# State products four in a row, a contiguous tap table stored from ScalarE's queue, and whole 128x128 turns of the state-space layer's input

## The chip, the cores and the metric

The kernel runs on one core of one Trainium2 chip. The metric is the device time of one execution in microseconds. The engines are named as in the profile: PE is TensorE's matmuls and PEld its weight loads, DVE is VectorE, ACT is ScalarE, POOL is GpSimd, and SP is SyncE, which only issues DMAs here. A name with a q (ACTq, SPq) is the engine's queue of waits and DMA issues.

## What is computed

The program is a two-layer sequence model on 1024 tokens of 1024 features, in float32: an RWKV-7 layer, an MLP, a diagonal state-space layer (S5) with GELU and a gated linear unit, and an MLP, with a LayerNorm behind each. The change is in the S5 layer, which has 64 groups of 16 features, each with a complex diagonal state of 64:

```python
bu_re = einsum('tbgc,gpc->tbgp', u_c, bbar_re)      # input products
bu_im = einsum('tbgc,gpc->tbgp', u_c, bbar_im)
# s_t = abar * s_(t-1) + bu_t, complex, one abar for each group and state
y = einsum('tbgp,gcp->tbgc', s_re, cr_w) - einsum('tbgp,gcp->tbgc', s_im, ci_w)
y = gelu(y + x * d_skip)
z = y @ w_glu
out = z[..., :d] * sigmoid(z[..., d:])
```

## The kernel before

**Layout and order.** Features lie on the 128 partitions, in 8 tiles; the tokens are halved, and `hA` and `hB` are the 8 tiles of 512 tokens of either half. All large products (the MLPs, the projections, the gate) go through `dense`: each float32 weight tile comes by DMA (`wraw`), ScalarE casts it to a high part (`whi`, L148), VectorE subtracts the rest (`wlo`, L149), and TensorE does three products per block (L188). The text calls this dense work. A list scheduler orders each engine's instructions by rank (`tc.cur_priority`): the S5 layer's steps have ranks from 99000 to 99500, the MLPs 200000. So while S5 of one half waits for something, dense work of the MLP of the other half goes first in TensorE's row. PSUM tiles come from four pools: `pd` (3 buffers, dense work), `pl` (1), `pa` (2) and `pc` (2).

**S5 in blocks of 8 tokens.** The recurrence is unrolled over blocks of 8 tokens, so that a half has 64 blocks (`NSC`) and a group's 16 features by 8 tokens fill 128 rows. `s5_tables` works out three tables for each of the 8 feature tiles, once, and stores them in DRAM: `tB` (input of a block to the state at its end), `tC` (state at a block's start to the block's outputs) and `tT`, the taps (inputs of a block to outputs of the same block). The taps of a tile are worked out in `pk`, copied by ScalarE into `kpad` behind zeros (L1155), and stored by SP with one overlapping read for each parity (L1159); a group's parity (`par`) is whether it is even or odd.

`s5(H, h)` then runs for each half in three stages.

- Input stage, by pairs of feature tiles (`f2` of 4): the tile's tokens are turned, 64 blocks at a time, by `turn` (L154 is a product by the identity, L156 a transpose), copied to `u1`, turned back by groups (L1195) to `ug`, multiplied by `tB` (L1206) and copied into the states `hb`.
- Scan: `advance` on VectorE and GpSimd, over `hb`.
- Output stage, by the same pairs: for each parity, the taps (L1250) and the state products (L1255) add into one PSUM tile `py`; ScalarE copies it to `y1` (L1257); TensorE turns it to features by tokens (`pyt`, L1263); VectorE adds the skip term (L1265) into `yg`, which has one buffer; ScalarE does GELU (L1267), and SP stores it to DRAM, where `glu` reads it.

A transpose writes a product's operand times the identity. In names such as `py<-tcm,hb 64*64 64x128`, `tcm` is the operand that moves through the array and `hb` the one loaded as weights, 64 rows by 64 columns; a product's column half follows from the output's partitions.

## Time and profile before

| | us |
|---|---|
| median of 3 runs | 2743.06 (2741.53 to 2747.41) |
| the profiled execution | 2746.6 |
| its span in the trace | 2744.8 |
| S5 tables | about 1070 to 1275 |
| first half: input stage, scan, output stage | about 1325 to 1410, 1410 to 1484, 1484 to 1540 |
| second half: input stage, scan, output stage | about 1858 to 1935, 1935 to 2010, 2010 to 2069 |

The span is that of the profiled execution from its first to its last instruction. The stages' ends are read from the timeline, where the first half's work begins and ends; dense work runs in all of them.

### The profile page before, as it was taken

The numbers are of one execution on the slowest core, as the hardware profiler recorded it, in microseconds if no ns is written. First come the engines' busy times: TensorE is split into PE (matmuls) and PEld (weight loads), VectorE is DVE, ScalarE is ACT, GpSimd is POOL, SyncE is SP. The second block draws the span as 40 slices with busy tenths as digits, with TensorE's granted clock in tenths as the row PEclk, the third lists the DMA queues.
The fourth block names the chain that finished last, engine by engine and source line by source line (L and its number), as shares of the span: only waits on it lengthen the run. The fifth ranks groups of instructions, "written<-read, shape, count | busy, mean of one in ns | idle before, by whom it ended". The sixth has DMA issues, their size and how long they took to land.

```text
span 2744.8 us, 43807 instructions
## 1 busy us (share of the span) xinstructions
PE 2598.4 (95%) x16582; PEld 2089.9 (76%) x16582; DVE 1813.3 (66%) x3191; ACT 1154.8 (42%) x2038; POOL 630.6 (23%) x515
## 2 busy tenths in 40 slices
PE   7999979989899999989999999999999999999997
PEld 5778757678677777767876788778778887788886
DVE  7477677577786867997567553674855546755556
ACT  7455574544543333353532332434223324433334
POOL 3121542432442122342122000120220101210101
PEclk9989979999899999999999999999999999999998
DMA  4765455564223334545333533233343322333333
GB/s 146 235 214 175 151 164 156 178 203 142 81 86 88 93 92 148 141 129 163 100 112 127 174 95 100 81 96 112 103 164 110 96 96 81 119 96 96 96 96 100
DMA packets 215058, 345.90 MB, mean 126 GB/s; under 512 B 21184, under 2 KB 75584, under 8 KB 214848
## 3 DMA queue, kind: packets, MB, share of 16 engines
q1 hardware_dynamic: 214848, 343.10, 40.5%
q8 instruction: 131, 2.15, 0.3%
q14 instruction: 79, 0.65, 0.1%
HBM read 279.06 MB, written 63.96 MB: 125 GB/s over the span
## 4 chain that ended last, share of the span: by engine, by line
PE 44%; DVE 4%; issue 3%; DMA 1%; POOL 1%; ACT 1%; ACTq 0%; SPq 0%; DVEq 0%; POOLq 0%
PE d L188 39%; PE py L1250 1%; PE py L1255 1%; DVE wlo L149 1%; DMA wraw<-in_mw_dram 1%; PE pu L154 1%; PE pbu L1206 1%; POOL rl L975 1%; DVE hA L991 0%; DMA s_y<-yg 0%; DVE t L1218 0%; DVE hB L991 0%; ACT whi L148 0%; DVE sq L876 0%; PE pu L1195 0%
## 5 line engine op out<-in xcount | busy, mean ns | idle before, releaser
L148 ACT CAST whi<-wraw 128x512 fp32r<-128x512 f32 x668 | 413.5, 620 | 929.1 <-PE d L188 623.2
L149 DVE TENSOR_TENSOR wlo<-wraw,whi 128x512 fp32r<-128x512 f32 x668 | 500.6, 750 | 426.8 <-ACT whi L148 404.3
L188 PE MATMUL d<-qbuf,whi 128*128 128x512 f32 (+1 forms) x2112 | 657.0, 394 | 23.8 <-DVE hA L991 12.8
L188 PEld LDWEIGHTS d<-qbuf,whi 128*128 128x128 f32 x2112 | 391.8, 191 | 120.0 <-DVE hA L991 17.8
L188 PE MATMUL d<-qbuf,wlo 128*128 128x512 f32 (+1 forms) x1056 | 411.9, 392 | 10.7 <-DVE wlo L149 10.4
L975 POOL TENSOR_TENSOR rl<-rl 128x512 f32<-128x512 f32 x128 | 157.2, 1228 | 1094.5 <-ACT rl L974 1094.5
L188 PE MATMUL d<-oAh,whi 128*128 128x512 f32 (+1 forms) x960 | 390.9, 411 | 15.5 <-ACT ev L418 6.3
L188 PE MATMUL d<-oAl,whi 128*128 128x512 f32 (+1 forms) x960 | 387.5, 405 | 3.0 <-DVE oAl L149 2.8
L188 PE MATMUL d<-oAh,wlo 128*128 128x512 f32 (+1 forms) x960 | 386.5, 405 | 2.4 <-DVE wlo L149 2.3
L188 PE MATMUL d<-oBh,whi 128*128 128x512 f32 x704 | 279.2, 397 | 0.0
L188 PE MATMUL d<-oBh,wlo 128*128 128x512 f32 x704 | 278.7, 396 | 0.2 <-DVE wlo L149 0.2
L188 PE MATMUL d<-oBl,whi 128*128 128x512 f32 x704 | 277.1, 394 | 0.0
L188 PEld LDWEIGHTS d<-qbuf,wlo 128*128 128x128 f32 x1056 | 201.7, 191 | 56.5 <-DVE wlo L149 14.5
L188 PEld LDWEIGHTS d<-oAh,whi 128*128 128x128 f32 (+1 forms) x960 | 185.9, 194 | 62.2 <-ACT ev L418 8.4
L188 PEld LDWEIGHTS d<-oAh,wlo 128*128 128x128 f32 (+1 forms) x960 | 185.8, 194 | 44.4 <-DVE wlo L149 3.2
L188 PEld LDWEIGHTS d<-oAl,whi 128*128 128x128 f32 (+1 forms) x960 | 185.6, 194 | 43.1 <-DVE oAl L149 5.2
L991 DVE TENSOR_TENSOR hB<-hB,d 128x512 f32<-128x512 f32 (+1 forms) x256 | 165.0, 650 | 71.2 <-PE d L188 68.0
L991 DVE TENSOR_TENSOR hA<-hA,d 128x512 f32<-128x512 f32 x240 | 162.1, 682 | 64.4 <-PE d L188 62.1
L188 PEld LDWEIGHTS d<-oBh,wlo 128*128 128x128 f32 x704 | 132.9, 189 | 32.4 <-issue 2.0
L188 PEld LDWEIGHTS d<-oBl,whi 128*128 128x128 f32 x704 | 133.1, 189 | 29.9 <-issue 0.7
L188 PEld LDWEIGHTS d<-oBh,whi 128*128 128x128 f32 x704 | 133.1, 189 | 29.0 <-issue 1.2
L149 DVE TENSOR_TENSOR qbuf<-rl,qbuf 128x512 fp32r<-128x512 f32 x128 | 95.0, 742 | 73.5 <-ACT qbuf L148 73.5
(374 smaller groups left out, 3804.8 us busy)
## 6 DMA issues: line engine op xcount, KB each, us to landing
wraw<-in_mw_dram SPq DMA_DIRECT2D x520, 256.0 KB, 2.7
wraw<-in_glu_dram SPq DMA_DIRECT2D x64, 256.0 KB, 2.7
low<-wlo SPq DMA_DIRECT2D x52, 256.0 KB, 2.6
wlo<-low SPq DMA_DIRECT2D x52, 256.0 KB, 3.6
wraw<-in_wk_dram SPq DMA_DIRECT2D x32, 256.0 KB, 3.5
wraw<-in_wr_dram SPq DMA_DIRECT2D x32, 256.0 KB, 3.9
wraw<-in_wv_dram SPq DMA_DIRECT2D x32, 256.0 KB, 4.3
yl<-s_y SPq DMA_DIRECT2D x32, 256.0 KB, 3.1
```

What stands on the lines that cost most here:

```text
L148: S.copy(hi, src)
L149: (e or V).tensor_sub(lo, src, hi.bitcast(F32))
L154: PE.matmul(out, x, idt, start=True, stop=True)
L188: bulk.append((PE.matmul(p, w, x, **kw).ins, x.shape[-1]))
L975: G.tensor_mul(r, r, r)
L991: V.tensor_add(z, z, p)
L1206: PE.matmul(p[qs, g2, ri], tb[:, g2, ri, qs], u[:, 2 * g2 + par], start=True, stop=True)
L1250: PE.matmul(p[64 * j : 64 * j + 64, g2], ug[f][:, 2 * g2 + par], tv[:, par, g2], start=g2 == 0, stop=False, skip_group_check=True)
L1255: PE.matmul(p[64 * j : 64 * j + 64, g2], hb[qs, 4 * f + g2, ri, 0:NSC], tcm[qs, g2, ri], start=False, stop=ri == 1, skip_group_check=True)
```

## The change

It has four parts.

1. Input stage. Each tile of the pair is turned by four transposes of 128x128, with every fourth token in one (L1200 of the changed kernel); the way back is by products with a selection matrix `sel` of 128 x 2 x 64 that picks the even or the odd rows (L1207), 16 for each tile.
2. Tap table. `tT` has another layout, in which the 128 columns of a tap's moving operand lie one behind the other; before, they lay 4 elements apart. There are two `kpad` tiles, for four feature tiles each; the stores go out in two groups of 16, after the fourth and the eighth tile, and ScalarE's queue issues them (L1170) instead of SP's.
3. Output stage. Both parities have a PSUM tile at once, one from `pc` and one from `pa`. The taps of both come first (L1264). The state products (L1272) go by both parities and both tiles of the pair in turn, four on the four 64x64 quadrants of the array; `inorder` fixes this order.
4. `pyt` is taken from `pl` (1 buffer) instead of `pa` (2).

```diff
@@ -31,6 +31,7 @@
 LNG = (1, 3, 5)
 LNT = (2, 5)
 TB = 2
+TBF = 4
 LN8R = 400000
 MIXR = 100
 W0B = 5
@@ -126,6 +127,8 @@
     cmask = kp.tile([128, 8, L], F32, name="cmask")
     V.memset(cmask, 1.0)
     V.memset(cmask[:, :, 0:1], 0.0)
+    sel = cp.tile([128, 2, 64], F32, name="sel")
+    V.tensor_copy(sel, ident.rearrange("p (n e) -> p e n", e=2))
     mhalf = cp.tile([128, 64], F32, name="mhalf")
     V.memset(mhalf, -0.5)
 
@@ -180,6 +183,12 @@
                     SP.dma_start(low[key, k0], lo.bitcast(F32).rearrange("p k n -> p (k n)"))
             out += [(hi[:, k], lo[:, k]) for k in range(step)]
         return out
+
+    def inorder(prods):
+
+        for x, y in zip(prods, prods[1:]):
+            tc.add_manual_dep(y.ins, x.ins.name, mybir.DependencyInfo(
+                mybir.DependencyClass.NoSync, mybir.DependencyReason.DATA), reason="order")
 
     bulk, hops = [], []
     ST = getattr(nc, STE)
@@ -1019,7 +1028,7 @@
 
     SL = 8
     NSC = HT // SL
-    tT = dr.tile([KT, 128, 2, 512], F32, name="tT")
+    tT = dr.tile([128, 2, KT, 4, 128], F32, name="tT")
     tB = dr.tile([KT, 128, 4, 2, 128], F32, name="tB")
     tC = dr.tile([KT, 128, 4, 2, 128], F32, name="tC")
 
@@ -1102,10 +1111,12 @@
         V.tensor_sub(ci, ci, tq)
         V.tensor_mul(ci, ci, den)
 
-        kpad = pp.tile([128, 16, 16, 4], F32, name="kpad")
-        G.memset(kpad, 0.0)
+        kpads = [pp.tile([128, TBF, 4, 16, 16], F32, name=f"kpad{j}") for j in range(KT // TBF)]
+        for kpad in kpads:
+            G.memset(kpad[:, :, :, 0:8], 0.0)
         for f in range(KT):
             gs = slice(4 * f, 4 * f + 4)
+            kpad = kpads[f // TBF]
             bc = pp.tile([128, 2, 2, 4, 16], F32, tag="bc", name="bc", bufs=1)
             SP.dma_start(bc, A["s5bc"][f])
             bb = pp.tile([128, 2, 4, 16], F32, tag="bb", name="bb", bufs=1)
@@ -1152,11 +1163,13 @@
                                   ca[ps_, g2, ri, 0:8].rearrange("p t c -> p (t c)"), start=ri == 0, stop=ri == 1)
             for par in range(2):
                 ps_ = slice(64 * par, 64 * par + 16)
-                S.copy(kpad[ps_, 8:].rearrange("p t c g -> p g (t c)"), p[ps_])
-            tv = tT[f].rearrange("(s c) two n -> two c s n", c=16)
-            for par in range(2):
-                src = kpad[64 * par : 64 * par + 16, 1:9].rearrange("p t c g -> p (t c g)")
-                SP.dma_start(tv[par], bass.AP(src.tensor, src.offset, [src.ap[0], (64, SL), src.ap[1]]))
+                S.copy(kpad[ps_, f % TBF, :, 8:].rearrange("p g t c -> p g (t c)"), p[ps_])
+            if f % TBF == TBF - 1:
+                for par in range(2):
+                    for s in range(SL):
+                        S.dma_start(
+                            tT[16 * s : 16 * s + 16, par, f - TBF + 1 : f + 1].rearrange("c f g n -> c (f g) n"),
+                            kpad[64 * par : 64 * par + 16, :, :, 1 + s : 9 + s].rearrange("c f g t e -> c (f g) (t e)"))
 
             bs = pp.tile([128, 4, 2, 128], F32, tag="bs", name="bs", bufs=1)
             for hf in range(2):
@@ -1178,21 +1191,21 @@
             V.tensor_copy(hb[:, :, :, 0], carry[0])
         ug = []
         for f2 in range(4):
-            u1 = s5p.tile([128, 8, SL, 16], F32, tag="u1", name="u1", bufs=2)
-            for s2 in range(2):
+
+            u1 = s5p.tile([128, 2, 8, 4, 16], F32, tag="u1", name="u1", bufs=2)
+            for j in range(2):
                 p = pa.tile([128, 4, 128], F32, tag="a", name="pu1")
-                for j in range(2):
-                    src = h[2 * f2 + j].rearrange("p (c s) -> p c s", s=SL)
-                    for s in range(4):
-                        turn(p[64 * j : 64 * j + 64, s], src[:, :, SL - 1 - 4 * s2 - s], ident, j)
-                S.copy(u1[:, :, 4 * s2 : 4 * s2 + 4].rearrange("p g s c -> p s g c"),
-                       p.rearrange("p s (g c) -> p s g c", g=8))
+                src = h[2 * f2 + j].rearrange("p (m s) -> p s m", s=4)
+                for s in range(4):
+                    PE.transpose(p[:, s], src[:, 3 - s], ident)
+                S.copy(u1[:, j].rearrange("p g s c -> p s g c"), p.rearrange("p s (g c) -> p s g c", g=8))
             for j in range(2):
                 f = 2 * f2 + j
-                ps_ = slice(64 * j, 64 * j + 64)
                 p = pc.tile([128, HT], F32, tag="c", name="pu2").rearrange("p (g n) -> p g n", g=8)
                 for g in range(8):
-                    PE.transpose(p[:, g], u1[ps_, g].rearrange("p s c -> p (s c)"), ident[ps_, ps_])
+                    for e in range(2):
+                        PE.matmul(p[64 * (1 - e) : 64 * (1 - e) + 64, g], u1[:, j, g].rearrange("p s c -> p (s c)"),
+                                  sel[:, e], start=True, stop=True)
                 u = s5p.tile([128, 8, NSC], F32, tag="ug", name="ug", bufs=8)
                 S.copy(u, p)
                 ug.append(u)
@@ -1237,28 +1250,34 @@
             tabs = []
             for f in (2 * f2, 2 * f2 + 1):
                 tt = s5p.tile([128, 2, 512], F32, tag="tab", name="tt", bufs=4)
-                SP.dma_start(tt, tT[f])
+                SP.dma_start(tt.rearrange("p two (g n) -> p two g n", g=4), tT[:, :, f])
                 tcm = s5p.tile([128, 4, 2, 128], F32, tag="tab", name="tcm", bufs=4)
                 SP.dma_start(tcm, tC[f])
-                tabs.append((f, tt.rearrange("p two (n g) -> p two g n", g=4), tcm))
+                tabs.append((f, tt.rearrange("p two (g n) -> p two g n", g=4), tcm))
+
+
+            pp = [r.tile([128, HT], F32, tag=t, name="py").rearrange("p (g n) -> p g n", g=4)
+                  for r, t in ((pc, "c"), (pa, "a"))]
+            for g2 in range(4):
+                for par in range(2):
+                    for j, (f, tv, tcm) in enumerate(tabs):
+                        PE.matmul(pp[par][64 * j : 64 * j + 64, g2], ug[f][:, 2 * g2 + par], tv[:, par, g2],
+                                  start=g2 == 0, stop=False, skip_group_check=True)
+            prods = []
+            for g2 in range(4):
+                for ri in range(2):
+                    for j, (f, tv, tcm) in enumerate(tabs):
+                        for par in range(2):
+                            qs = slice(64 * par, 64 * par + 64)
+                            prods.append(PE.matmul(pp[par][64 * j : 64 * j + 64, g2], hb[qs, 4 * f + g2, ri, 0:NSC],
+                                                   tcm[qs, g2, ri], start=False, stop=ri == 1, skip_group_check=True))
+            inorder(prods)
             for par in range(2):
-                qs = slice(64 * par, 64 * par + 64)
-                p = pc.tile([128, HT], F32, tag="c", name="py").rearrange("p (g n) -> p g n", g=4)
-
-                for g2 in range(4):
-                    for j, (f, tv, tcm) in enumerate(tabs):
-                        PE.matmul(p[64 * j : 64 * j + 64, g2], ug[f][:, 2 * g2 + par], tv[:, par, g2],
-                                  start=g2 == 0, stop=False, skip_group_check=True)
-                for g2 in range(4):
-                    for ri in range(2):
-                        for j, (f, tv, tcm) in enumerate(tabs):
-                            PE.matmul(p[64 * j : 64 * j + 64, g2], hb[qs, 4 * f + g2, ri, 0:NSC], tcm[qs, g2, ri],
-                                      start=False, stop=ri == 1, skip_group_check=True)
-                S.copy(y1[:, :, :, par].rearrange("p t g c -> p g t c"), p.rearrange("p g (t c) -> p g t c", t=SL))
+                S.copy(y1[:, :, :, par].rearrange("p t g c -> p g t c"), pp[par].rearrange("p g (t c) -> p g t c", t=SL))
             for j in range(2):
                 f = 2 * f2 + j
                 js = slice(64 * j, 64 * j + 64)
-                p = pa.tile([128, SL, NSC], F32, tag="a", name="pyt")
+                p = pl.tile([128, HT], F32, tag="l", name="pyt").rearrange("p (t n) -> p t n", t=SL)
                 for t in range(SL):
                     PE.transpose(p[:, t], y1[js, t].rearrange("p g r c -> p (g r c)"), ident[js, js])
                 y = s5p.tile([128, HT], F32, tag="yg", name="yg", bufs=1)
```

How the rows of TensorE and ScalarE change is shown at three places. In the order, each product is one instruction.

**TensorE, input stage of the second pair of the first half.** `pu` is the PSUM tile that a turn writes, `d` dense work. Before:

```order
L156 MATMUL pu_13521<-ident,hA 64x128 x4
L154 MATMUL pu_13521<-ident,hA 64x128 x4
...
L156 MATMUL pu_13531<-ident,hA 64x128 x4
L154 MATMUL pu_13531<-ident,hA 64x128 x4
...
L188 MATMUL d<-qbuf,wlo 128x512
L1195 MATMUL pu_13541<-ident,u_13520 128x64 x8
L1195 MATMUL pu_13572<-ident,u_13520 128x64 x8
L188 MATMUL d<-qbuf,whi 128x512 x2
...
L1206 MATMUL pbu<-ug,tb 64x64 x32
```

After:

```order
L1200 MATMUL pu_13549<-ident,hA 128x128 x4
L197 MATMUL d<-oBh,whi 128x512
...
L1200 MATMUL pu_13555<-ident,hA 128x128 x4
L197 MATMUL d<-oBh,wlo 128x512
L1207 MATMUL pu_13561<-sel,u_13548 64x64 x16
...
L1207 MATMUL pu_13600<-sel,u_13548 64x64 x10
L1219 MATMUL pbu<-ug,tb 64x64 x16
L1207 MATMUL pu_13600<-sel,u_13548 64x64 x6
...
L1219 MATMUL pbu<-ug,tb 64x64 x16
```

The four half turns (L156 and L154, two visits) have become two visits of four whole ones (L1200), and the way back (L1195) is 32 products instead of 16, the second tile's in two pieces around the input products of the first.

**TensorE, output stage of the third pair of the first half.** `pyt` is the turn of the second pair's outputs, `py<-tt` are the third pair's taps and `py<-tcm` its state products. Before:

```order
L188 MATMUL d<-oBh,wlo 128x512
L1250 MATMUL py<-tt,ug 64x128
L1263 MATMUL pyt<-ident,y_13970 128x64 x16
L1250 MATMUL py<-tt,ug 64x128 x7
L1255 MATMUL py<-tcm,hb 64x128
L1250 MATMUL py<-tt,ug 64x128 x5
L1255 MATMUL py<-tcm,hb 64x128 x15
L1250 MATMUL py<-tt,ug 64x128 x3
L1255 MATMUL py<-tcm,hb 64x128 x16
```

After:

```order
L1282 MATMUL pyt<-ident,y_14022 128x64 x8
L1264 MATMUL py<-tt,ug 64x128 x14
L1272 MATMUL py<-tcm,hb 64x128 x8
L1282 MATMUL pyt<-ident,y_14022 128x64 x8
L1272 MATMUL py<-tcm,hb 64x128 x24
L197 MATMUL d<-qbuf,whi 128x512 x2
L197 MATMUL d<-qbuf,wlo 128x512
L1264 MATMUL py<-tt,ug 64x128 x2
```

The turn `pyt` is now in two pieces, the second behind 14 taps and 8 state products. The taps of both parities stand ahead of all 32 state products; the two in the last row belong to the fourth pair already.

**ScalarE, table stage, around the fourth feature tile.** `kpad<-pk` are the tap copies, `whi` the casts for dense work, `bs` the copies of the other table. Before:

```order
L1155 COPY kpad<-pk 16x4x128 x2
L148 CAST whi<-wraw 128x512
L1167 COPY bs<-pb_13098 128x512
L148 CAST whi<-wraw 128x512
L1167 COPY bs<-pb_13104 128x512
L148 CAST whi<-wraw 128x512
```

After:

```order
L1166 COPY kpad_12867<-pk 16x4x128 x2
L151 CAST whi<-wraw 128x512
L1170 DMA tT<-kpad_12867 16x16x128 x16
L1180 COPY bs<-pb_13110 128x512
L1180 COPY bs<-pb_13116 128x512
L151 CAST whi<-wraw 128x512 x2
L983 ACTIVATE rl<-d 128x512
L881 ACTIVATE sq_12054<-hB 128x512
```

A row of 16 DMA issues stands between the tile's tap copies and the copies of the other table.

## Rows read from the trace of the kernel before

**Rows 1.** Head of the page: span; busy time of each engine.

```profile
span 2744.8 us, 43807 instructions
PE 2598.4 (95%) x16582; PEld 2089.9 (76%) x16582; DVE 1813.3 (66%) x3191; ACT 1154.8 (42%) x2038; POOL 630.6 (23%) x515
```

**Rows 2.** Stretches: length, busy us (instructions) by engine, PEclk, DMA share, GB/s.

```profile
1325.00:1410.00 85.00, 85.00 (x679) 68.54 (x678) 38.99 (x58) 36.02 (x61) 11.76 (x9) 1.00 0.37 115
...
1490.00:1540.00 50.00, 50.00 (x434) 37.63 (x433) 21.37 (x29) 18.36 (x31) 2.09 (x2) 1.00 0.65 227
...
1858.00:1935.00 77.00, 76.96 (x634) 62.50 (x633) 35.32 (x53) 32.58 (x57) 7.14 (x6) 1.00 0.38 118
...
2020.00:2065.00 45.00, 45.00 (x402) 33.54 (x399) 17.66 (x23) 16.12 (x28) 2.10 (x2) 1.00 0.55 193
```

**Rows 3.** Stretches of the table stage, 1070 to 1300 us: their sum and mean.

```profile
sum 230.00, PE 209.41 PEld 161.41 DVE 205.06 ACT 94.33 POOL 75.15; mean PE 19.04 PEld 14.67 DVE 18.64 ACT 8.58 POOL 6.83
```

**Rows 4.** Timeline of TensorE, input stage: start, us, engine, line, operation, count.

```profile
1386.19 0.60 PE L156 MATMUL pu<-ident,hA 128*64 128x128 f32 x4
1386.72 1.23 PE L154 MATMUL pu<-ident,hA 128*64 128x128 f32 x8
1387.87 0.50 PE L188 MATMUL d<-qbuf,wlo 128*128 128x512 f32 x1
...
1394.23 1.01 PE L1195 MATMUL pu<-ident,u 64*128 64x64 f32 x16
```

**Rows 5.** Timeline of TensorE, input products of one pair of tiles.

```profile
1343.73 2.09 PE L1206 MATMUL pbu<-ug,tb 128*64 128x64 f32 x64
```

**Rows 6.** Timeline of TensorE, three places in the first layer.

```profile
108.21 1.10 PE L573 MATMUL pb<-rksel,kf 64*64 64x1 f32 x32 [1.28 <-POOL E L549]
...
421.08 1.71 PE L596 MATMUL pA<-AR,KB 64*128 64x128 f32 x16
...
914.95 1.17 PE L596 MATMUL pA<-AR,KB 64*128 64x128 f32 x16
916.05 1.09 PE L609 MATMUL pT<-ident,KB 128*128 128x128 f32 x8
916.90 0.48 PE L188 MATMUL d<-oAh,whi 128*128 128x512 f32 x1
917.21 0.39 PE L188 MATMUL d<-oAl,whi 128*128 128x512 f32 x1
```

**Rows 7.** Instructions by line: count, duration ns min/median/max, first and last start.

```profile
L154 PEld LDWEIGHTS pu<-ident,hA x64: 194/209/220, 1328.3 to 1390.5; 128*64 128x64 f32 x64
...
L1206 PE MATMUL pbu<-ug,tb x512: 222/222/271, 1343.7 to 1931.1; 128*64 128x64 f32 x171
...
L1250 PE MATMUL py<-tt,ug x256: 388/406/422, 1401.4 to 2055.1; 128*64 128x128 f32 x128
...
L1255 PE MATMUL py<-tcm,hb x512: 269/269/473, 1481.2 to 2057.2; 64*64 64x128 f32 x171
```

**Rows 8.** Timeline of TensorE, output stage of one pair of tiles.

```profile
1492.49 1.96 PE L1255 MATMUL py<-tcm,hb 64*64 64x128 f32 x32
1494.38 2.01 PE L1250 MATMUL py<-tt,ug 128*64 128x128 f32 x16
1496.33 1.96 PE L1255 MATMUL py<-tcm,hb 64*64 64x128 f32 x32
```

**Rows 9.** Timeline of VectorE in the output stage.

```profile
1494.35 1.19 DVE L1265 SCALAR_TENSOR_TENSOR yg<-hA,pv,pyt 128x512 f32<-128x512 f32 x1 [2.82 <-DMA s_y<-yg]
```

**Rows 10.** Instructions by line in the table stage.

```profile
L1159 SPq DMA_DIRECT2D tT<-kpad x16: 320/362/1264, 1128.6 to 1268.9; - x16
...
L1155 ACT COPY kpad<-pk x16: 1055/1074/1087, 1126.9 to 1267.7; 16x512 f32<-16x512 f32 x16
...
L1167 ACT COPY bs<-pb x16: 566/587/591, 1129.1 to 1272.9; 128x512 f32<-128x512 f32 x16
```

**Rows 11.** The page's costliest groups: ScalarE's weight casts.

```profile
L148 ACT CAST whi<-wraw 128x512 fp32r<-128x512 f32 x668 | 413.5, 620 | 929.1 <-PE d L188 623.2
```

## The prediction

> **What bounds the kernel now.** I read the head of the page first: TensorE is busy 2598.4 of 2744.8 us [rows 1], so the question is in which stretches it is full. The table by stretches answers it. In the state-space layer's input stage (1325 to 1410 us for the first half of the tokens, 1858 to 1935 for the second) and in its output stage (1490 to 1540 and 2020 to 2065) TensorE is busy for 85.00 of 85, 76.96 of 77, 50.00 of 50 and 45.00 of 45 us, while VectorE and ScalarE work less than half the time [rows 2]. The products of the MLP fill every gap there, so a microsecond of small matmuls saved in these four stretches is a microsecond of dense work earlier. The granted clock is 1.00 in all four, so the change isn't weighed at a lower clock. The scan between them is VectorE's and is not edited. The stage that builds the tables is another matter: over 230 us VectorE is busy 205.06, TensorE 209.41, ScalarE 94.33 [rows 3].
>
> **Input stage.** Before, each pair of feature tiles gets two visits of four transposes and four ordinary products by the identity, then 16 small transposes. The timeline shows a visit from 1386.19 to 1387.87, 1.68 us, and the 16 transposes in 1.01 [rows 4]: 2 x 1.68 + 1.01 = 4.37 us. After, there are 8 whole transposes and 32 products with the selection matrix, which run as 64 records, since each fp32 product that is no transpose leaves two (here 4 such products leave 8 records). The second have the shape that the input products (L1206) already have: 128 rows, 64 weight columns, 64 moving columns, alternating column halves; 64 of those took 2.09 us [rows 5]. For the transposes there are two bounds. Eight 128x128 transposes of contiguous weights took 916.90 - 916.05 = 0.85 us [rows 6]; if the strided weights have to be loaded one after the other, the 209 ns of L154's strided load [rows 7] gives 8 x 0.209 = 1.67. L154's own records, strided too, follow at (1387.87 - 1386.72) / 8 = 0.144 us, so I take 8 x 0.144 = 1.15. After: 2.09 + 1.15 = 3.24, a gain of 1.13 per pair, and there are 4 pairs in each of 2 halves: **-9 us** (ends -4.9 and -11.4).
>
> **Taps.** Sixteen records take 1496.33 - 1494.38 = 1.95 us [rows 8], and there are 16 such visits (4 pairs, 2 parities, 2 halves): 31.2 us. One of those records lasts 406 ns; a state product with the same 64x128 output lasts 269 [rows 7]. Two things differ: 128 contraction rows instead of 64, and a moving operand whose elements lie 16 bytes apart. The rows aren't the reason as far as the trace goes: L1206 has 128 rows too, and lasts 222 ns for 64 columns [rows 7]. So I put the excess on the stride, which the new table removes. At the state products' pace, 1.89 / 32 = 0.059 us a record [rows 8], a visit takes 0.95 and 16.1 us are saved; at twice L1206's 0.033 for twice its columns, 1.05 and 14.4. I take **-15**; the lower end is 0, if the 128 rows together with 128 columns cost it.
>
> **State products.** Sixteen visits of 32 records in 1.89 us (1492.49 to 1494.38) [rows 8] are 30.2 us. Here only the column half alternates; the row half stays for a whole visit. Now each group of four covers the four quadrants, rows alternating, in two PSUM banks. Evidence on alternating row halves: L596 at 421.08, four of one row half, then four of the other, needs 1.71 us for 16 records; at 914.95, row halves alternating record by record, the same 16 take 1.17 [rows 6]. So row halves do overlap, as column halves do (0.059 against 0.107 a record). Whether both overlap at once no row shows. The lower bound for one 64x64 weight tile with hardly any columns behind it is L573: 32 in 1.10 us, 0.034 each [rows 6]. 512 x 0.034 = 17.6, a gain of 12.6; halving the pace of now would gain 15.1. I take **-13**; if fours run as two pairs it is 0. The Trainium skill (TensorE: Matmul & The Clock Gate, Part 3: Packing small matmuls) says that a weight load overlaps running matmuls only where the row group differs, and that products at different tile positions start some 4 ns apart. The 1.17 against 1.71 agrees with the first half; that L1255's records, all of one row half, already run at 0.059 does not. Taken alone the rule would price the products of before at one after the other and those of after at four at once, an estimate of 128 x (0.107 + 0.012) = 15 us for all, much as the halved pace gives.
>
> **Switches.** In the order of both halves TensorE changes between dense and small work 48 times instead of 56 in the input stages and 30 instead of 16 in the output stages. The dense record behind small ones shows 0.48 us at 916.90, the next 0.39 [rows 6]: about 0.09 each, 6 more: **+0.5**.
>
> **The output transposes' buffer.** They move to a pool with one buffer, so the second of a pair waits for VectorE's pass over the first, 1.19 us [rows 9]. Between the two the order puts 12 to 14 taps, and up to 8 state products, at least 24 x 0.059 = 1.4 us, which covers it: 0. Without that cover 8 pairs x 1.2 = +10. VectorE's pass itself waits 2.82 us for the store of the tile before it [rows 9], about 4 us a tile and 8 a pair, below the 50 / 4 = 12.5 us that a pair takes now; even 4.5 less would leave 8.
>
> **Table stage.** The 16 tap stores leave SP's queue (median issue 362 ns, longest 1264 [rows 10]) and become 2 bursts of 16 on ScalarE's, which stands still meanwhile: 16 x 0.362 = 5.8 us a burst, about 9 if the later ones, which wait for lanes or for the burst's own earlier stores, take longer. Queued behind are the two table copies of that tile and the weight casts, for which VectorE's subtractions and then TensorE's dense products wait. Against it stands that ScalarE works 94.33 of 230 us [rows 3], that SP has 16 issues less, that 16 copies of 1.07 us [rows 10] write contiguous runs (0.59 is what a contiguous copy of 512 columns to 128 partitions, L1167, takes there [rows 10]), and that a burst meets a weight tile that was cast before it: 668 casts in the span [rows 11] are one in 4.1 us. Of 5.8 to 9 us a burst, 1.7 to 4.9 are left, and I take 2.5: **+5**; ends 0 and 2 x 9 = +18. The two larger zero fills lie on GpSimd, busy 75.15 of 230 [rows 3], before the first copy: 0. The Trainium skill (DMA: Bandwidth & Descriptors, Issuing engines are not separate DMA queues) says that a second issuing engine saves only the issue time, since all share the same 16 engines. It speaks against this move: SP's 5.8 us are the most to gain, and ScalarE pays them. No run here shows it yet.
>
> **Sum.** -9 - 15 - 13 + 0.5 + 5 = -31.5 us. The profiled execution took 2746.6, 3.5 above the median of the three runs, 2743.06; I apply the difference to the median: 2711.6, say **2712**.
>
> **Rivals.**
> - Fours run as two pairs, the state products gain nothing: -18.5, **2724.5**. For it: no row shows four at once. Against: either half alternating alone does overlap, and the load bound is 0.034. Chance 0.16.
> - ScalarE's bursts reach TensorE in full, +18 instead of +5: -18.5, **2724.5**. For it: casts feed everything, VectorE is nearly full. Against: ScalarE's 59% of idle time. Chance 0.09.
> - The change doesn't do what it says for the taps (the stride was not the cause): -16.5, **2726.5**. Chance 0.06.
> - Slower: in fours, with both the row half and the column half changing, each record waits for the one before, as in L596's 1.71 / 16 = 0.107 [rows 6]. Then the state products take 512 x 0.107 = 54.8 instead of 30.2, +24.6, and the sum is -9 - 15 + 24.6 + 5.5 = +6: **2749**. It decides from 0.095 a record on (0.059 + 18.5 / 512). For it: four writes into the same columns of one bank pair each. Against: 1.17 at 914.95. Chance 0.05.
> - The saved time is lost again, as the dense work moved out of these stages meets VectorE's full stretches: within 5 us of **2743**. Against: only 5% of TensorE's time is idle anywhere [rows 1]. Chance 0.04.
>
> My forecast keeps 0.60. 0.2% is 5.5 us, about what a measurement of this kernel can tell from no change. Slower by more than that needs the fourth rival, 0.05; within it are the fifth and what is left of double mishaps, 0.07; faster 0.88. The range goes from all favourable ends (-11.4 - 16.1 - 15.1 + 0.5 = -42, 2701) to just beyond the three middle rivals: 2702 to 2730.
>
> **What the new profile would show.** Input stage: the selection products at about 2.1 us per 64 records, four transposes in 0.45 to 0.8. Taps: records of 270 ns instead of 406, 16 of them in 0.95. State products: 64 of a pair in 2.1 to 2.3 us; 3.8 is the first rival, near 7 the fourth. Table stage: two rows of 16 DMA issues on ScalarE's queue near 1170 and 1270 us, with no cast for 6 to 9 us, and TensorE or VectorE idle behind them for more or less than 5 us together. The forecast is wrong most likely by the state products' pace or by that idle time.

## The result, and the profile after

The changed kernel took 2751.31 us (median of 20 runs, 2741.45 to 2759.3), the kernel before 2740.1 (20 runs, 2723.77 to 2747.41): a ratio of 1.0043, with a 95% interval of 1.0032 to 1.0055. I had forecast 2712, faster. It is slower, by some 12 us.

The two profiles have to be read with care, since the profiled execution of after, 2743.4, is one of its fastest and that of before, 2746.6, one of its slowest. The page of after, head and busy times, to be set against [rows 1]:

```profile
span 2741.7 us, 44312 instructions
PE 2558.9 (93%) x16838; PEld 2069.5 (75%) x16838; DVE 1824.3 (67%) x3192; ACT 1144.4 (42%) x2038; POOL 635.8 (23%) x516
```

TensorE works 39.5 us less, yet the span is only 3.1 us shorter. And part of that has nothing to do with the change. The last instruction of a line in the first layer, which the change doesn't touch, starts at 982.9 us before and at 973.4 after (instructions by line: durations, first and last start):

```profile
L660 PE MATMUL pv<-XT,x x512: 191/191/258, 228.6 to 982.9; 32*32 32x32 f32 x171
```

```profile
L669 PE MATMUL pv<-XT,x x512: 191/191/258, 231.5 to 973.4; 32*32 32x32 f32 x171
```

So from there on the changed kernel loses 9.5 - 3.1 = 6.4 us in this pair. To see where, I took the starts of successive TensorE records between two marks that both kernels have, the last transpose of the tables (L1166 of before) and the last tanh of the second half's gate (L1013), and split the time: 0.2274 us for each dense record, the time up to the next start for the small ones, the gaps (where a start comes more than 0.26 us late, or over 0.6 us after a small record), and the rest, dense records that run slower, at a lower clock or behind a switch. Dense work is 832.7 us in every kernel; the other three, in us of one profiled execution each, with the ratio to the kernel before from the timed rounds:

| kernel | length | small | gaps | slower | ratio (95%) |
|---|---|---|---|---|---|
| before | 1012.6 | 137.4 | 24.3 | 18.4 | 1 |
| after | 1019.2 | 97.8 | 61.0 | 27.9 | 1.0043 (1.0032 to 1.0055) |
| input_stage_only | 1008.5 | 126.4 | 29.1 | 20.6 | 0.9989 (0.9975 to 1.0002) |
| output_stage_only | 1011.9 | 125.7 | 35.7 | 18.0 | 1.0014 (1.0003 to 1.0025) |
| tap_table_only | 1024.2 | 124.8 | 44.0 | 23.0 | 1.0042 (1.0028 to 1.0056) |
| table_stores_spread | 999.3 | 118.8 | 29.9 | 18.1 | 0.9968 (0.9954 to 0.9983) |
| no_tap_table | 1003.8 | 115.0 | 34.2 | 22.2 | 0.9973 (0.9957 to 0.9989) |
| repaired | 1001.0 | 98.5 | 45.4 | 24.6 | 0.9965 (0.9949 to 0.9981) |
| taps_loaded_first | 998.0 | 100.6 | 42.2 | 22.8 | 0.9948 (0.9927 to 0.9969) |
| first_pair_no_limits | 993.7 | 99.1 | 42.6 | 19.6 | 0.9926 (0.9914 to 0.9938) |

The small products became 39.6 us cheaper, and 36.7 us of gaps and 9.5 of slower records took their place: +6.6, about half of the timed difference. In this table the change in length of a single execution and the change in the timed rounds differ by up to some 5 us. Of the added gaps, about 14 lie between the tables and the input stage, 1.9 behind the first turns of that stage, and about 16 in the two output stages between the first `pyt` and the last.

That TensorE's part came as forecast is seen by line. Before, the taps, the state products and `pyt` (count | busy us, mean ns | idle time before them):

```profile
L1250 PE MATMUL py<-tt,ug 128*64 128x128 f32 x256 | 40.4, 408 | 0.0
...
L1255 PE MATMUL py<-tcm,hb 64*64 64x128 f32 x512 | 32.5, 275 | 0.0
...
L1263 PE MATMUL pyt<-ident,y 64*128 64x64 f32 x128 | 8.1, 229 | 0.0
```

After:

```profile
L1264 PE MATMUL py<-tt,ug 128*64 128x128 f32 x256 | 21.6, 282 | 10.6 <-DMA tt<-tT 10.6
...
L1207 PE MATMUL pu<-sel,u 128*64 128x64 f32 x512 | 20.1, 225 | 2.3 <-ACT u L1201 2.3
...
L1272 PE MATMUL py<-tcm,hb 64*64 64x128 f32 x512 | 17.3, 273 | 0.0
...
L1282 PE MATMUL pyt<-ident,y 64*128 64x64 f32 x128 | 11.3, 229 | 1.3 <-ACT y L1276 1.1
```

Taps 40.4 to 21.6 us, state products 32.5 to 17.3. And the last column has something new: TensorE waits 10.6 us for tap tables. The stretches of after, in the order of [rows 2]:

```profile
1262.00:1275.00 13.00, 4.55 (x22) 3.40 (x20) 2.75 (x4) 0.00 (x0) 0.00 (x0) 0.81 0.77 100
1275.00:1290.00 15.00, 10.52 (x38) 8.54 (x39) 7.05 (x12) 3.97 (x7) 1.04 (x1) 0.71 0.85 228
1330.00:1400.00 70.00, 68.31 (x732) 56.04 (x732) 34.92 (x52) 32.97 (x56) 4.19 (x4) 1.00 0.35 115
1480.00:1490.00 10.00, 7.75 (x51) 5.67 (x50) 6.92 (x8) 4.53 (x7) 4.25 (x3) 0.83 0.47 162
1490.00:1500.00 10.00, 7.74 (x97) 6.09 (x96) 2.39 (x4) 2.94 (x5) 0.00 (x0) 1.00 0.88 289
1500.00:1510.00 10.00, 7.78 (x119) 5.96 (x118) 4.97 (x7) 2.84 (x5) 0.00 (x0) 0.95 0.70 240
```

The input stage is nearly full (68.31 of 70), but ahead of it 13 us hold 4.55 of work, at a granted clock that falls to 0.71 in the next stretch, and in the output stage TensorE works 7.75 of 10 us, with the DMA engines busy 0.88 and 0.70 of two of the stretches.

What happens near 1262 us is on ScalarE's timeline (ACTq is its queue, with the DMA issues):

```profile
1257.77 1.18 ACT L1166 COPY kpad<-pk 16x512 f32<-16x512 f32 x2 [0.56 <-PE pk L1162]
1258.37 1.60 ACTq L1170 DMA_DIRECT2D tT<-kpad  x2
1258.97 0.59 ACT L1180 COPY bs<-pb 128x512 f32<-128x512 f32 x1
1260.01 17.79 ACTq L1170 DMA_DIRECT2D tT<-kpad  x14
1277.84 0.59 ACT L1180 COPY bs<-pb 128x512 f32<-128x512 f32 x1 [18.28 <-DMA tT<-kpad]
...
1278.81 1.14 ACT L151 CAST whi<-wraw 128x512 fp32r<-128x512 f32 x2
```

Fourteen issues take 17.79 us, and the weight cast comes behind them. TensorE's timeline beside it:

```profile
1266.16 0.39 PE L197 MATMUL d<-qbuf,wlo 128*128 128x512 f32 x1
1279.48 2.93 PE L197 MATMUL d<-qbuf,whi 128*128 128x512 f32 x6 [12.93 <-ACT whi L151]
```

### The profile page after: what moved, and what is told of

Same layout as the page of the kernel before. It is cut to its first block, busy times and chain, and to the rows that moved or that the text cites. A ratio compares the mean times of both kernels' runs of the same rounds, so it can differ in the third digit from the quotient of the medians.

```text
span 2741.7 us, 44312 instructions
## 1 busy us (share of the span) xinstructions
PE 2558.9 (93%) x16838; PEld 2069.5 (75%) x16838; DVE 1824.3 (67%) x3192; ACT 1144.4 (42%) x2038; POOL 635.8 (23%) x516
## 4 chain that ended last, share of the span: by engine, by line
PE 55%; DVE 15%; issue 5%; DMA 5%; ACT 3%; POOL 2%; ACTq 1%; SPq 0%; DVEq 0%; POOLq 0%
PE d L197 49%; DVE wlo L152 3%; ACTq L1170 1%; DMA wraw<-in_mw_dram 1%; PE pA L605 1%; DVE hA L1000 1%; DMA yl<-s_y 1%; ACT whi L151 1%; PE pu L1207 1%; DVE xh L650 1%; DVE t L1231 1%; PE pbu L1219 1%; DVE x L648 1%; DMA lda<-s_a 1%; DVE qbuf L152 1%
## 5 line engine op out<-in xcount | busy, mean ns | idle before, releaser
L152 DVE TENSOR_TENSOR wlo<-wraw,whi 128x512 fp32r<-128x512 f32 x668 | 509.6, 764 | 418.1 <-ACT whi L151 403.2
```

The source lines that it names most:

```text
L152: (e or V).tensor_sub(lo, src, hi.bitcast(F32))
```

## The experiments

All were timed in five rounds beside the kernel before on the same chip; the table above has the ratios that are not given here. Some kernels were timed on different chips, so they are compared with each other by these ratios.

**stores_on_sp.** Edit to the changed kernel:

```diff
-                        S.dma_start(
+                        SP.dma_start(
                             tT[16 * s : 16 * s + 16, par, f - TBF + 1 : f + 1]...
```

> The changed kernel with its 32 tap stores issued by SP instead of ScalarE. Theory 1 (the time lost in the table stage, about 18 us, is ScalarE standing still at its own DMA issues): casts go on, TensorE does not wait 13 us for whi near 1266 us, and the time is 12 to 18 us below the changed kernel, about 2735. Rival (the stores' 512-byte pieces hold up whatever queue issues them): SP stands instead, the weight loads come late, TensorE waits as long for whi behind wraw, and the time stays within 4 us of the changed kernel's 2751.

It took 2758.54 us, a ratio of 1.0052 (1.0032 to 1.0071): the rival by the ratio, which is 1.0043 for after, though 7 us above the 2751 that it named. SP's timeline, and ScalarE's longest wait there (us in total, times, longest):

```profile
1269.71 19.51 SPq L1170 DMA_DIRECT2D tT<-kpad  x16
```

```profile
ACT whi L151 <- DMA wraw<-in_mw_dram: 21.4, 2, 21.2
```

SP stands 19.5 us, and the cast that stood behind ScalarE's issues now stands 21.2 us for a weight load behind SP's; TensorE waits 14.2 us for that cast. The queue isn't what costs; the burst is. The issues of after show it, against a median of 362 ns in [rows 10]:

```profile
L1170 ACTq DMA_DIRECT2D tT<-kpad x32: 309/1309/2467, 1160.3 to 1276.2; - x32
```

**tap_table_only**, the kernel before with part 2 of the change alone.

> The kernel before with the tap table's part alone, stored from ScalarE's queue. Theory 1: +14 to +18 from the burst near 1270 us, and the taps' 14 us saved on TensorE come back only where the output stages do not wait for anything else: between +0 and +18, about 2748. Rival (my forecast): -10, 2730.

2756.16 us: theory 1, the whole loss. TensorE waits 12.3 us for one cast there.

**table_stores_spread**, the kernel before with a contiguous table and other stores:

```diff
-        kpad = pp.tile([128, 16, 16, 4], F32, name="kpad")
+        kpad = pp.tile([128, 4, 16, 16], F32, name="kpad")
...
-                SP.dma_start(tv[par], bass.AP(src.tensor, src.offset, [src.ap[0], (64, SL), src.ap[1]]))
+                for g in range(4):
+                    src = kpad[64 * par : 64 * par + 16, g, 1:9].rearrange("p t c -> p (t c)")
+                    SP.dma_start(tv[par][:, :, 128 * g : 128 * g + 128],
+                                 bass.AP(src.tensor, src.offset, [src.ap[0], (16, SL), src.ap[1]]))
```

> The kernel before with a contiguous tap table, but stored by SP after each tile, 8 stores of 64 KB in 512-byte pieces for each tile, instead of two bursts of 2 MB. Theory 1 (the burst is what costs, since 2 MB of such pieces land at some 120 GB/s behind one queue and nothing else gets on): no wait for whi of more than 3 us in the table stage, taps 14 us cheaper on TensorE, half of that kept: 2733 to 2740. Rival (512-byte pieces cost the same wherever they stand): +10 or more, 2753.

2734.05 us, theory 1. The same bytes in the same 512-byte pieces, behind each tile (instructions by line), and the stretch in which after stood still:

```profile
L1160 SPq DMA_DIRECT2D tT<-kpad x64: 325/430/2002, 1129.1 to 1271.9; - x64
```

```profile
1255.00:1275.00 20.00, 19.33 (x111) 15.04 (x110) 15.20 (x24) 8.63 (x15) 2.56 (x2) 1.00 0.58 146
```

The median issue is 430 ns, TensorE is busy 19.33 of 20 us. Against tap_table_only the spreading is worth 0.74%, some 20 us, and this part alone is a gain of 0.32%. Two more things differ between the two kernels. SP issues the stores, which gained nothing in stores_on_sp. And a tile's table lies in one piece in DRAM, so that a load reads runs of 4 KB instead of 2 KB; TensorE's wait for the taps, 10.6 us in after and 11.5 in the repaired kernel below, shows no gain from that. The taps in this run, in the order of before and with the new table, against 40.4 us and 408 ns:

```profile
L1252 PE MATMUL py<-tt,ug 128*64 128x128 f32 x256 | 22.5, 281 | 1.8 <-DMA tt<-tT 1.8
```

**repaired** is the changed kernel with these stores, **no_tap_table** the changed kernel with the table of before.

> All three parts, with the table stored by SP after each tile as in the run beside it. Theory 1: without the burst the changed kernel's 2751 falls by 12 to 18, to 2733 to 2739; TensorE idles 5 to 9 us in each output stage, which keeps it from the 2707 that the three prices alone would give (2743 - 9 - 15 - 14 + 2). Rival: 2707 to 2712.

> The input stage's and the output stage's part together, the tap table as before. Theory 1 (what TensorE saves there is mostly given back, because the chain of table loads, copies and VectorE's sums then sets the pace of the output stage): 0 to -6, 2738 to 2744, TensorE idle 4 to 9 us in each output stage. Rival (TensorE's prices add up, -9 - 15): about 2720.

2732.6 and 2734.68 us: both as theory 1 has it, or a little better, and far from the rivals. Without the burst the change is a gain of 0.35%, about 10 us; TensorE's small work is 38.9 us less than before.

**input_stage_only** and **output_stage_only**, one part each on the kernel before.

> The kernel before with the input stage's part alone. My forecast gave -9 us for it. If TensorE's time in the input stage counts one for one: -6 to -9, about 2732 to 2734. Rival (the two input stages are held by the chain of copies and table loads as soon as TensorE has less to do): 0 to -4, and TensorE shows idle time in the input stage, for u behind ScalarE's copies or for dense work behind VectorE.

> The kernel before with the output stage's part alone (state products four in a row, one-buffer pyt), table as before. TensorE's price: 64 state products of a pair in 1.95 us instead of 3.8, -15 us in all. If that counts: about 2726. Rival (the output stage then waits for the loads of its tables, 2 MB a pair into four buffers): 0 to -5, and TensorE waits for tt or tcm by DMA for 4 to 8 us in each output stage.

2742.27 and 2747.79 us. The first is the rival, though its ratio can't be told from no change. TensorE waits once in each input stage, behind its first turns, in the first half for VectorE's sums and in the second for ScalarE's copy (us in total, times, longest):

```profile
PE d L190 <- DVE hB L991: 1.8, 1, 1.8
```

```profile
PE pu L1195 <- ACT u L1189: 1.3, 1, 1.3
```

The second is slower than even its rival, which had 0 to -5 us, and TensorE waits 3.2 and 2.9 us for taps in the two output stages, less than the 4 to 8 that the rival named. By line:

```profile
L1255 PE MATMUL py<-tt,ug 128*64 128x128 f32 x256 | 39.8, 409 | 6.1 <-DMA tt<-tT 6.1
...
L1263 PE MATMUL py<-tcm,hb 64*64 64x128 f32 x512 | 18.6, 275 | 0.6 <-DVE hb L1228 0.6
...
L1273 PE MATMUL pyt<-ident,y 64*128 64x64 f32 x128 | 11.3, 228 | 2.3 <-ACT y L1267 2.2
```

The state products are as cheap as in after, 18.6 us instead of 32.5, and nothing of it is left: TensorE waits 6.1 us for tap tables and 2.3 at `pyt`, where the kernel before shows 0.0.

**one_pairs_tables**, to the changed kernel:

```diff
-            tabs = []
+            if f2 == 0:
+                kept = []
+            tabs = kept
             for f in (2 * f2, 2 * f2 + 1):
+                if f2 > 0:
+                    continue
...
```

> The changed kernel, in whose output stages the tables of the first pair of tiles serve all four pairs: 12 of 16 loads of each output stage, 6 MB, and the waits for them are left out. Theory 1 (the output stage waits for its table loads): TensorE no longer waits for tt, both output stages end 6 to 9 us earlier, the time is 12 to 18 below the changed kernel's, 2733 to 2739. Rival (VectorE's and ScalarE's chain over yg, the casts and the sums of the dense work set the pace): 0 to -5, 2746 to 2751, and the idle time moves to DVE hB, ACT rl or ACT y.

2745.69 us, 1.001 (0.9992 to 1.0028), some 9 us below the changed kernel by the ratios: between the two. The wait for tables is gone, and another has its place:

```profile
L1269 PE MATMUL py<-tt,ug 128*64 128x128 f32 x256 | 21.3, 310 | 0.0
...
L1288 PE MATMUL pyt<-ident,y 64*128 64x64 f32 x128 | 12.5, 245 | 14.6 <-DVE yg L1290 8.2 <-ACT y L1282 6.4
```

**taps_loaded_first, two_buffer_pyt, both_output_edits.** Edits to the repaired kernel in short form, the third kernel with both:

```diff
-            for f in (2 * f2, 2 * f2 + 1):
-                SP.dma_start(tt, tT[f]); SP.dma_start(tcm, tC[f])
+            for f in fs: SP.dma_start(tts[f], tT[f])
+            for f in fs: SP.dma_start(tcs[f], tC[f])
```

```diff
-                  for r, t in ((pc, "c"), (pa, "a"))]
+                  for r, t in ((pc, "c"), (pl, "l"))]
...
-                p = pl.tile([128, HT], F32, tag="l", name="pyt")
+                p = pa.tile([128, SL, NSC], F32, tag="a", name="pyt")
```

> The repaired kernel (all three parts, table stored tile by tile) with both tap tables of a pair loaded ahead of both state tables, so that the next pair's taps take the buffers that the taps of this pair leave, and don't stand behind a state table that waits for this pair's last state product. Theory 1 (TensorE's idle time in the output stages is the wait for the tap loads): the waits for tt, 4.4 us in either stage, go, and the time falls by 4 to 8 us below the repaired kernel's 2733, to 2725 to 2729. Rival (the loads together are what takes long, 2 MB a pair): the wait moves to tcm, the time stays within 3 us.

> The repaired kernel with two pools exchanged: pyt back in the pool with two buffers, the second parity's py in the one with one. Theory 1 (loads of taps): 0 to -3 against the repaired kernel's 2733, since TensorE there waited for pyt's buffer hardly at all. Rival (the single buffer of pyt sets the pace of the output stage through VectorE's yg): -6 to -10, 2723 to 2727.

> The two edits beside it together. When the tap loads no longer wait, the run with the first pair's tables showed what comes next: TensorE waiting for pyt's buffer (3.6 and 4.6 us) and for ScalarE's y (2.7 and 3.7). Theory 1: both edits together take 8 to 12 us from the repaired kernel, 2721 to 2725. Rival: the order of the loads alone gives the same.

2728.66 us, as theory 1 has it; 2737.06 (0.9981, 0.9968 to 0.9994), a little slower than either expectation, in an interval that overlaps the repaired kernel's; and 2735.77 (0.9973, 0.9959 to 0.9987). The taps and `pyt` in the repaired kernel, then with the taps loaded first, then with two buffers for `pyt`:

```profile
L1258 PE MATMUL py<-tt,ug 128*64 128x128 f32 x256 | 22.5, 294 | 11.5 <-DMA tt<-tT 11.5
...
L1276 PE MATMUL pyt<-ident,y 64*128 64x64 f32 x128 | 11.3, 229 | 1.7 <-ACT y L1270 1.4
```

```profile
L1263 PE MATMUL py<-tt,ug 128*64 128x128 f32 x256 | 22.9, 310 | 0.3 <-PE py L1271 0.2
...
L1281 PE MATMUL pyt<-ident,y 64*128 64x64 f32 x128 | 11.9, 237 | 9.6 <-DVE yg L1283 6.0 <-ACT y L1275 3.1 <-DVE hb L1188 0.5
```

```profile
L1258 PE MATMUL py<-tt,ug 128*64 128x128 f32 x256 | 21.1, 288 | 15.3 <-DMA tt<-tT 15.3
...
L1276 PE MATMUL pyt<-ident,y 64*128 64x64 f32 x128 | 8.7, 240 | 1.3 <-ACT y L1270 1.3
```

Loading the taps first takes their wait from 11.5 to 0.3 us, and `pyt`'s grows from 1.7 to 9.6. Two buffers for `pyt` do the reverse, 15.3 and 1.3. The first is the fastest complete kernel here, though its interval overlaps the repaired one's; the third is no better than the first, and my expectation of 8 to 12 us for both edits fell.

**first_pair_no_limits, ring_yg, ring_yg_two_pyt.** In all three `yg` comes from the ring of `ug` (`tag="ug", bufs=8`); the first is otherwise the repaired kernel with one pair's tables and exchanged pools, the second has the taps loaded first, the third that and the exchanged pools.

> The repaired kernel, with the tables of the first pair used for all four pairs of an output stage (12 of 16 loads left out), pyt in the pool with two buffers, and yg in the ring of the eight ug buffers. Theory 1 (the three waits are what takes the saved time): TensorE idles under 2 us in either output stage, and the time is 12 to 18 below the repaired kernel's 2733, 2715 to 2721. Rival (the casts, sums and relu of the dense work set the pace there): the idle time moves to DVE hB, ACT rl, and at most 6 us are won, 2727 or more.

> The kernel with the taps loaded first, and yg in the ring of ug's buffers instead of its one, so that VectorE's pass doesn't wait for the store of the tile before. Theory 1: the 9.6 us for which TensorE waited there at pyt, 6.0 of them for VectorE's yg, shrink by 4 to 6, and the time falls by 3 to 6 below that kernel's 2729. Rival: no change, the wait goes to ScalarE's y or back to the loads.

> The same with the two pools exchanged as well. Theory 1: as the run beside it within 3 us, or slower, since the early tap of the next pair stands again at its load (12.3 us in the kernel with both output edits). Rival (pyt's single buffer was the limit): 4 us or more faster than the run beside it.

2723.73, 2730.57 (0.9954, 0.9941 to 0.9967) and 2731.3 us (0.9953, 0.9938 to 0.9968): the two with complete work are no faster than with the taps loaded first alone. With all three waits taken away the gain is 0.0039 of the time over the repaired kernel, about 11 us, less than theory 1 wanted and more than its rival. The waits went on to ScalarE's copy of `y`:

```profile
L1263 PE MATMUL py<-tt,ug 128*64 128x128 f32 x256 | 22.0, 302 | 5.1 <-ACT y L1276 5.1
...
L1282 PE MATMUL pyt<-ident,y 64*128 64x64 f32 x128 | 8.8, 242 | 5.5 <-ACT y L1276 5.5
```

With `yg` in the ring alone, `pyt` still waits:

```profile
L1281 PE MATMUL pyt<-ident,y 64*128 64x64 f32 x128 | 11.3, 228 | 8.6 <-ACT y L1275 4.8 <-DVE yg L1283 3.8
```

**input_and_spread** (input stage and spread table, output stage as before) and **output_side_loads_first** (taps_loaded_first without the input stage's part).

> The kernel before with the input stage's part and the contiguous table stored tile by tile; the output stage's order as before. Theory 1 (state products four in a row gain nothing because the output stage then waits, and the two other parts add up): as fast as all three or faster, 2729 to 2733. Rival (the three parts share one limit): slower than the repaired kernel, 2736 to 2740.

> The kernel with the taps loaded first, without the input stage's part. Theory 1 (the input stage's part saves 8 us of TensorE's time and less than half of that on the clock): 0 to 4 us slower than with it, 2729 to 2733. Rival (all of it counts once the output stage doesn't wait): 7 to 9 us slower, 2736 to 2738.

2739.46 (0.9983, 0.9966 to 1.0) and 2745.5 us (1.0, 0.9989 to 1.0012): the rivals, the second by more than it had said. The input stage's part adds nothing to the spread table, yet without it the kernel with the taps loaded first has no gain at all. I can't put the parts into one sum.

## Why the prediction was wrong

**TensorE's prices were right.** Input stage: -9 forecast; the small records from the tables to its end, both halves, fall from 60.9 to 52.2 us, -8.7. Taps and state products with the switches: -27.5 forecast; the stretches of scan and output stage fall from 76.5 to 45.6, -30.9. The first rival (fours run as two pairs) and the fourth (one after the other) are refuted by the timeline of after:

```profile
1483.56 0.71 PE L1282 MATMUL pyt<-ident,y 64*128 64x64 f32 x8 [1.06 <-ACT y L1276]
...
1488.32 1.80 PE L1264 MATMUL py<-tt,ug 128*64 128x128 f32 x26
1490.05 0.71 PE L1282 MATMUL pyt<-ident,y 64*128 64x64 f32 x8
1490.69 0.43 PE L1264 MATMUL py<-tt,ug 128*64 128x128 f32 x2
1491.05 1.98 PE L1272 MATMUL py<-tcm,hb 64*64 64x128 f32 x64
1492.96 0.73 PE L197 MATMUL d<-qbuf,whi 128*128 128x512 f32 x2
1495.95 0.65 PE L1264 MATMUL py<-tt,ug 128*64 128x128 f32 x4 [2.26 <-DMA tt<-tT]
```

Sixty-four state products in 1.91 us are 0.030 each, and 26 taps in 1.73 are 0.067, nearest to the estimate from twice L1206. The estimate from the Trainium skill (TensorE: Matmul & The Clock Gate, Part 3: Packing small matmuls), 15 us for all state products, stands against 8 pairs x 1.91 = 15.3 by this timeline and 17.3 of busy time. That the stride had cost the taps, the third rival's question, is shown by table_stores_spread: 408 ns a record before, 281 there, in the same order.

**The table stage's term was mis-sized.** I had +5, with +18 as a rival's end: about 14 us of gaps and 1.8 of slower records came, 16 in all. (The 1.9 us of gaps behind the first turns of the input stage are not the burst's: input_stage_only and repaired have 2.0 there.) The failed step is "16 x 0.362 = 5.8 us a burst, about 9 if the later ones ... take longer". I priced issues; what a burst takes is the landing of 2 MB in small pieces. The 16 stores of the second burst land one behind the other from 1261.8 to 1283.1 us, some 1.4 us apart, and the later issues go out at about that pace. Bursts of 19.64 and 17.79 us, in after, are twice my upper figure. The Trainium skill's rule that the prediction cites (DMA: Bandwidth & Descriptors, Issuing engines are not separate DMA queues) agrees with stores_on_sp: another queue gained nothing. The first burst, at 1161 us, did little harm, for TensorE waited there 8.1 us for ScalarE where it had waited for VectorE's tables before. The second had only dense work beside it. So the second rival's +18 was near, but by luck: one burst cost it, twice as long as I had it, and not two.

**The main step failed: "a microsecond of small matmuls saved in these four stretches is a microsecond of dense work earlier".** TensorE was full there before; that doesn't say that what stood behind it had slack. Without the burst, 38.9 us saved gave 11.6 on the length (1012.6 to 1001.0), and 0.35% in the timed rounds. Most of the rest went into the output stages. Here they are from the first state product to the last turn, either half, before and then in the repaired kernel, in the order of [rows 2]:

```profile
1481.20:1533.70 52.50, 52.50 (x495) 39.63 (x494) 20.13 (x27) 18.75 (x31) 7.48 (x5) 1.00 0.65 229
2010.00:2062.50 52.50, 52.50 (x495) 39.75 (x494) 20.50 (x27) 17.90 (x31) 7.49 (x5) 0.99 0.57 201
```

```profile
1466.60:1522.70 56.10, 49.00 (x516) 38.83 (x516) 25.67 (x33) 20.13 (x35) 8.57 (x5) 0.94 0.69 230
1990.60:2049.90 59.30, 49.43 (x514) 38.99 (x514) 27.49 (x34) 18.92 (x34) 9.29 (x6) 0.91 0.58 186
```

With less small work and some more dense work in them, these stretches became longer, not shorter. Counting waits of over 0.15 us, TensorE stands in them for 16.7 us where it stood for nothing: 11.5 for tap tables, 2.8 for ScalarE's `y` and `rl` (the MLP's activation), 2.4 for VectorE's sums of dense work. In the input stages it stands for 3.0 us, where it stood for nothing; in the scans for 15.1, much as before (14.7). The timeline of after, above, shows one place: the early taps of the third pair start at 1495.95, after TensorE has waited 2.26 us for their table, and dense products stand behind them in its fixed order, which then run without a wait. Before, a pair's small products took longer, and no tap waited for its table. The fifth rival ("the saved time is lost again") had 0.04 and named VectorE; it should have named the loads first, and behind them `pyt`'s buffer and ScalarE's copies. The measured 2751 is this failure together with the burst's, and no rival had both; "Slower by more than that needs the fourth rival" fell with them.

**One term of mine held only by accident.** "The output transposes' buffer: 0" is right in after (1.3 us, most of it for ScalarE's copy), while the table loads hold the stage. Where they don't and the buffer is single, TensorE waits 8.6 to 14.6 us at `pyt`, of which 3.8 to 8.2 are for VectorE's `yg`, that is for the buffer.

**What stays open.** Which limit comes last in the output stage isn't settled: tables, `pyt`'s buffer, `yg` and ScalarE's `y` take each other's place, and with the first three gone 7 us of the lost 27 come back by the length (1001.0 to 993.7), some 11 by the timed ratios. Nor is it settled why the input stage's part is worth 0.1% by itself (in an interval that includes nothing), nothing beside the spread table, and 0.5% beside both others; each edit also gives the scheduler another order of dense work, and no run held that order fixed.

## What to carry to other kernels

An engine that is 100% busy with filler work is not thereby the limit of the stage: before pricing a saving at one for one, look at what the saved time had been hiding (loads into a full ring of buffers, a single PSUM buffer, the copies between two products), and ask how late each would be if the engine came earlier. Count a batch of stores by when it lands, not by its issues, and leave it spread if anything else shares its queue. Change one part at a time: here one part's loss hid the others' gain.

## What the runs showed of the hardware

- Products on the four 64x64 quadrants, in two PSUM banks, run at 0.030 us each, against 0.059 where only the column half alternates; before, no row showed four at once.
- A moving operand with elements 16 bytes apart made a 128-column fp32 record last 408 ns on average; contiguous, 281 in the same order (table_stores_spread).
- Bursts of 16 stores of 128 KB in 512-byte pieces took 18 to 20 us on either queue, about 14 x 128 KB / 17.8 us = 103 GB/s; 64 KB stores in the same pieces, eight behind each tile, issued at a median of 430 ns and landed in a median of 2.6 us. While the second burst of after went out and SP issued nothing (1262 to 1275 us), the DMA engines were busy 0.77 at 100 GB/s; from 1490 to 1500, 0.88 at 289.
- TensorE stood for 12.93 us, from 1266.55 to 1279.48. The granted clock, 1.00 from 1240 to 1262, was at its lower level (0.50, 1.2 GHz) from 1275 to 1279, and 1.00 again from 1285 to 1290; over 1275 to 1290 its mean was 0.71.
